# All cache pages fetched from the SP queue with the page number in a register

## The chip, the cores and the metric

The kernel runs on one core of a Trainium2 chip. The metric is the device time of one execution in microseconds (us); lower is better. Three runs of the kernel before gave 2349.99, 2351.92 and 2353.11 us, median 2351.92 us.

The engines are named as the profile names them: PE multiplies matrices (PEld is its weight load), DVE and ACT work element by element, POOL is the fourth compute engine, and SP computes nothing: its instruction queue (SPq) issues nearly all transfers between the chip's memory and the on-chip buffer. Every queue runs its instructions in order, so an instruction that waits holds up all that stands behind it on the same queue.

## What is computed

One step of a decoder layer for a prompt of 512 positions and 8 samples of 4 positions (544 columns together). The input is normalized and multiplied by one large projection; three branches (pooling, attention, state space) follow, each is projected back, and the results are gated, merged and projected out.

The change concerns the attention of the samples. Each sample has 2048 earlier positions in a paged cache: 16 pages of 128 positions, at places that a table of page numbers gives.

```python
past = cache_kv[l][page_table].reshape(bd, past_len, N_KV_ROWS, N_KV_HEADS, HEAD_DIM)
...
kc = jnp.einsum('bnlkd,lde->bnke', blk[:, :, :, 0] + pe_cmp[0][:, None, :], w_phi[0])
vc = jnp.einsum('bnlkd,lde->bnke', blk[:, :, :, 1] + pe_cmp[1][:, None, :], w_phi[1])
...
ss = jnp.einsum('bqkgd,bkqjcd->bkgqjc', qx, kg).astype(f32) * scale
...
o_sel = jnp.einsum('bkgqjc,bkqjcd->bqkgd', ps.astype(vg.dtype), vg)
```

A page has four tables: two for the compressed keys and values (`c0`, `c1`), and keys and values for the selected blocks (`ck`, `cv`). So 8 samples x 16 pages x 4 tables = 512 page fetches of 128 rows x 1 KB (128 KB) each.

## The kernel before

The dense work is a list of units, each one 128x1024 block of weights. `step` (L167) runs one unit: first it takes one turn of each background generator, then the evacuation of the previous unit, then `w_split` of the unit two ahead (ACT makes a rounded copy `whi` of the raw weights `wr`, DVE the rest `wlo`, L144 and L145), then `w_load` (L133: SP fetches the 512 KB of a unit three beyond that into one of 3 buffers `wr`), and then the unit's matmuls: 48 in a unit of the input projection, three for each product (L149 to L151). The kernel is scheduled by hand: every queue gets its instructions in the order in which the Python code issues them.

The attention work is one long background generator, taken in turns by the steps. Two of its parts read the cache, both through `gather(dst, table, col)`, where `col` numbers the 128 pages:

- `g_compress` (L604) goes through 16 jobs (8 samples, keys and values). A job's tile `ca` holds 16 pages; there are two such tiles. In three steps a job does 2 x 32 pairs of small matmuls (L632), and the pages of the next job (6, 5 and 5 of them in the three steps) are fetched into the other tile.
- `g_decode` (L1286) works through 20 chunks: for each of 4 pairs of samples four chunks of four cached pages per sample, and one chunk of the window, which is no paged fetch (L1307, L1318). For keys `gk` and values `gv` there are 4 buffers each, which is two chunks. `get_k` is called behind the score matmuls of a chunk (L1431) and fetches two chunks ahead; `get_v` is called behind the matmuls with the values (L1514) and does the same. A chunk with pages is 8 fetches. In the middle of the decode one step has both: 16 fetches.

`gather` splits the pages: an odd page goes over SP (L585 loads the page number from the on-chip row `PT` into a register, L586 issues a plain transfer whose address uses it), an even page goes over POOL as an indirect DMA (L589), which reads one row number for each partition from the table `IDX`. `make_idx` (L592) builds `IDX` at the start: POOL an iota, SP a transfer of the page table to all partitions, DVE four conversions.

In the SP queue a step's fetches stand ahead of the step's `w_load`, since the background turn comes first.

Of the kernel before, what the change touches and what calls it, by code (L numbers as in the profile page):

```python
# [10 lines left out]
F32 = mybir.dt.float32  # L11
F32R = mybir.dt.float32r
I32 = mybir.dt.int32
AF = mybir.ActivationFunctionType
OP = mybir.AluOpType
# [13 lines left out]
NPOOL = 160  # L29
# [37 lines left out]
def kernel(ctx, tc, a):  # L67
    nc = tc.nc
    pe, dve, act, pool, sp = nc.tensor, nc.vector, nc.scalar, nc.gpsimd, nc.sync
    ctx.enter_context(tc.manual_schedule())  # L70

    def P(name, bufs=1, **kw):
        return tc.tile_pool(name=name, bufs=bufs, **kw)
# [5 lines left out]
    consts = ctx.enter_context(P("consts"))  # L79
# [36 lines left out]
    ones = consts.tile([128, 128], F32, name="ones")  # L116
    epsb = consts.tile([128, 1], F32, name="epsb")

    # ---------------------------------------------------------------- dense stream
    raw, whi, wlo = {}, {}, {}  # L120
    lo_eng = [dve]
    early = [False]
# [36 lines left out]
    state = {"u": 0}  # L159
# [37 lines left out]
            fn()  # L197
            mid.pop(0)

    # ---------------------------------------------------------------- start: x, first weights  # L200
    xr_s = ExitStack()
    xr_p = xr_s.enter_context(P("xr"))
    XH, XL, XR = [], [], []
    first = wraw_p.tile([128, 8, 128], F32, name="wr")
# [98 lines left out]
            after.append(lambda hf=hf: rms_spread(hf))  # L303
        xr_s.close()

    # ---------------------------------------------------------------- pools of the first part
    att_s = ExitStack()
    kc_p = att_s.enter_context(P("kc", side="right"))
    KC = kc_p.tile([128, 2, 8, 64], F32, name="kc")
# [3 lines left out]
    KN = kc_p.tile([128, 2, 2, 32], F32, name="kn")  # L313
    GQ = kc_p.tile([128, 4, 48], F32, name="gq")

    # ---------------------------------------------------------------- evacuation of in-projection tiles
    done = set()
    sub = {}

# [256 lines left out]
                later(lambda t=t, i=2 * gi + md: sp.dma_start(ypool[i], t))  # L576
        step(u, mms, evac)

    # ---------------------------------------------------------------- compressed keys and values
    IDX = consts.tile([128, 128], I32, name="idx")  # L580
    PT = consts.tile([1, 128], I32, name="ptrow")

    def gather(dst, table, col):
        if col % 2:
            r = sp.value_load(PT[0:1, col:col + 1], min_val=0, max_val=NPOOL - 1)  # L585
            sp.dma_start(dst, a[table].rearrange("(g p) x -> g p x", p=128)[bass.ds(r, 1)]  # L586
                         .rearrange("g p x -> (g p) x"))
        else:
            pool.indirect_dma_start(out=dst, out_offset=None, in_=a[table],  # L589
                                    in_offset=bass.IndirectOffsetOnAxis(ap=IDX[:, col:col + 1], axis=0))  # L590

    def make_idx():  # L592
        pi = consts.tile([128, 1], I32, name="pidx")
        pool.iota(pi, pattern=[[0, 1]], base=0, channel_multiplier=1)
        pf = consts.tile([128, 1], F32, name="pidxf")
        dve.tensor_copy(pf, pi)
        sp.dma_start(PT, a["pt"])
        sp.dma_start(IDX, a["pt"].to_broadcast([128, 128]))
        f = consts.tile([128, 128], F32, name="idxf", bufs=1)
        dve.tensor_copy(f, IDX)  # L600
        dve.tensor_scalar(f, f, 128.0, pf, op0=OP.mult, op1=OP.add)
        dve.tensor_copy(IDX, f)

    def g_compress():  # L604
        with ExitStack() as s:
# [8 lines left out]
            def fetch(n, pages):  # L614
                if n >= len(jobs):
                    return
                b, k = jobs[n]
                if n not in tiles:
                    tiles[n] = cap.tile([128, 16, 256], F32, name="ca")
                for pg in pages:  # L620
                    gather(tiles[n][:, pg, :], f"c{k}", b * 16 + pg)
# [52 lines left out]
                dve.tensor_scalar(KCP[:, k, :16], KCP[:, k, :16], KCP[:, k, 16:17], None, op0=OP.add)  # L674
                dve.tensor_scalar(KC[:, k], KC[:, k], KCP[:, k, 16:17], None, op0=OP.add)

    # ---------------------------------------------------------------- state space
    SSM = {}
    par_s = ExitStack()

# [343 lines left out]
        par_s.close()  # L1024
        done.add("ssm")

    # ---------------------------------------------------------------- attention of the prompt
    def g_prompt():
        while not all(("q", i) in done for i in range(8)):
            yield  # L1030
# [251 lines left out]
        s.close()  # L1282
        done.add("prompt")

    # ---------------------------------------------------------------- attention of the samples
    def g_decode():  # L1286
        s = ExitStack()
        dp = s.enter_context(R("dec", 2))
# [10 lines left out]
        def get_k(r, c):  # L1299
            for b2 in range(2):  # L1300
                b_ = 2 * r + b2
                t = gp.tile([128, 4, 2, 128], F32, name="gk")
                if c < 4:
                    for pg in range(4):
                        gather(t[:, pg].rearrange("q p t -> q (p t)"), "ck", b_ * 16 + c * 4 + pg)
                else:
                    sp.dma_start(t.rearrange("q a b c -> q (a b c)"), a["wkT"][b_].rearrange("q p t -> q (p t)"))  # L1307
                kt[r, c, b2] = t

        def get_v(r, c):  # L1310
            for b2 in range(2):
                b_ = 2 * r + b2
                t = gp.tile([128, 4, 256], F32, name="gv")
                if c < 4:
                    for pg in range(4):
                        gather(t[:, pg], "cv", b_ * 16 + c * 4 + pg)
                else:
                    sp.dma_start(t, a["wv"][b_])  # L1318
                vt[r, c, b2] = t
# [222 lines left out]
        s.close()  # L1542
        done.add("decode")

    # ---------------------------------------------------------------- operands of the branches
    YH, YL = {}, {}
    yps = {}

# [59 lines left out]
                yz[k] = (y, z)  # L1608
            yield

    # ---------------------------------------------------------------- run the first part
    make_idx()

    def g_copy():
        while "ssm" not in done:
# [58 lines left out]
            fn()  # L1674
    xs.close()

    # ---------------------------------------------------------------- branches
    acc_p = ctx.enter_context(P("accp", 17))
    lg_p = ctx.enter_context(P("lgp", 3))
    xo_p = ctx.enter_context(P("xo", 24))  # L1680
# [157 lines left out]
    normalize(1, range(16))  # L1838


# ------------------------------------------------------------------------------ host side
def col_lists():
    off = np.cumsum([0, 1024, 1024, 1024, 1536, 48, 1024, 1024, 1024, 6144])
    pu, pz, q, kv, ag, az, su, sz, mg = off[:9]
    hd = []
    for p in range(2):
        for g in range(4):
            hd.append(np.concatenate([((2 * p + k) * 4 + g) * 64 + np.arange(64) for k in range(2)]))
    ssm = []
    for i in range(8):  # L1850
        c, g = np.meshgrid(np.arange(2 * i, 2 * i + 2), np.arange(64), indexing="ij")
        ssm.append((g * 16 + c).reshape(-1))
    agc = []
    for j in range(3):
        for p in range(2):
            for g in range(4):
                for k in range(2):
                    agc.append(((2 * p + k) * 4 + g) * 3 + j)
    r = np.arange(128)
    return dict(hd=hd, ssm=ssm, cols={  # L1860
        "pu": [pu + 128 * i + r for i in range(8)], "pz": [pz + 128 * i + r for i in range(8)],
        "q": [q + h for h in hd], "az": [az + h for h in hd],
        "kv": [kv + 128 * i + r for i in range(12)],
        "ag": [ag + np.array(agc + [agc[0]] * 80)],
        "su": [su + s for s in ssm], "sz": [sz + s for s in ssm],
        "mg": [mg + 128 * i + r for i in range(48)]})
# [138 lines left out]
```

## Time and profile before

| | |
|---|---|
| median of the timed runs | 2351.92 us (2349.99 to 2353.11) |
| span of the profiled execution | 2475.4 us |
| PE busy | 2345.3 us, 95% of the span |
| DVE, ACT, POOL busy | 1111.0, 652.3, 419.9 us |
| mean granted clock of PE | 0.965 |
| POOL's indirect DMAs | 256 |
| SP's page fetches | 256 |

No other time than the span is recorded for the profiled execution. The span is 123.5 us longer than the median of the timed runs. A row of a timeline gives the start, how long, the queue or engine, the line, the operation, what was written from what, how many were merged (x4), and in brackets the idle time before it and what ended it. "issue" is idle time for which the profile shows nothing that was waited for. In a row of the windows view each engine's busy time is followed by the number of its instructions, then come the granted clock (PEclk), the DMA share and GB/s.

### The profile page before, as it was taken

Reading aid. Unit: us, or ns where it says so; the run is one execution under the profiler, and the core shown is the slowest. Engines: PE = TensorE matmul, PEld = TensorE weight load, DVE = VectorE, ACT = ScalarE, POOL = GpSimd, SP = SyncE. Lnnn points to the kernel's source line nnn. Section 1 sums busy time; section 2 is a strip of 40 time slices with the busy share of each in tenths; the row PEclk is TensorE's granted clock in tenths of the full one; section 3 lists DMA queues with packets and bytes.
Section 4 is the critical chain, followed back from the end, with each engine's and each line's share of the span. In section 5 each row is a group of like instructions: output and inputs, shape, how many; then the busy total and the mean of one; then the engine's idle time right before and its main releaser. Section 6 shows DMA issues by size and latency. Waiting matters only on the chain.

```text
span 2475.4 us, 49565 instructions
## 1 busy us (share of the span) xinstructions
PE 2345.3 (95%) x20454; PEld 2236.5 (90%) x20454; DVE 1111.0 (45%) x2157; ACT 652.3 (26%) x1117; POOL 419.9 (17%) x387
## 2 busy tenths in 40 slices
PE   8888888999978999999999999889999999999995
PEld 7888888899978999999999898779999999999995
DVE  6223334114498324676666333322452545554225
ACT  5101111112311111444544222222342222222331
POOL 3122222213235200000000214551000001200003
PEclk9898989999999999999999999999999999999998
DMA  7554564546323666533333357775553555443332
GB/s 241 153 128 125 136 165 124 149 120 137 106 80 108 143 195 195 168 91 96 100 92 87 121 156 246 239 220 170 189 136 118 170 194 191 145 131 111 113 110 91
DMA packets 271650, 358.32 MB, mean 145 GB/s; under 512 B 136129, under 2 KB 186050, under 8 KB 271042
## 3 DMA queue, kind: packets, MB, share of 16 engines
q1 hardware_dynamic: 259138, 321.60, 44.0%
q0 software_dynamic: 12288, 33.57, 4.9%
q8 instruction: 161, 2.64, 0.4%
q14 instruction: 63, 0.52, 0.1%
HBM read 309.26 MB, written 54.13 MB: 147 GB/s over the span
## 4 chain that ended last, share of the span: by engine, by line
PE 89%; DVE 5%; issue 4%; DMA 1%; SPq 0%; ACT 0%; POOL 0%; DVEq 0%; POOLq 0%; ACTq 0%
PE d L149 25%; PE d L151 23%; PE d L150 23%; PE s L632 5%; PE o L1244 2%; PE s L1180 2%; PE t L1220 2%; PE o L1514 1%; DVE t L902 1%; DVE sh L905 1%; PE s L1431 1%; DVE t L904 1%; PE s L963 1%; DVE t L903 1%; PE s L974 1%
## 5 line engine op out<-in xcount | busy, mean ns | idle before, releaser
L149 PE MATMUL d<-xh,whi 128*128 128x272 f32 x3424 | 1022.2, 299 | 24.4 <-DVE e L324 13.4
L151 PE MATMUL d<-xl,whi 128*128 128x272 f32 x3424 | 998.3, 292 | 9.0 <-issue 8.7
L150 PE MATMUL d<-xh,wlo 128*128 128x272 f32 x3424 | 998.1, 291 | 4.5 <-issue 4.0
L149 PEld LDWEIGHTS d<-xh,whi 128*128 128x128 f32 x3424 | 659.7, 193 | 55.7 <-issue 33.2
L151 PEld LDWEIGHTS d<-xl,whi 128*128 128x128 f32 x3424 | 658.9, 192 | 9.1 <-issue 8.0
L150 PEld LDWEIGHTS d<-xh,wlo 128*128 128x128 f32 x3424 | 659.9, 193 | 5.7 <-issue 5.0
L145 DVE TENSOR_TENSOR wlo<-wr,whi 128x1024 fp32r<-128x1024 f32 x298 | 376.8, 1265 | 302.6 <-ACT whi L144 292.9
L144 ACT ACTIVATE whi<-wr 128x1024 fp32r<-128x1024 f32 x309 | 323.0, 1051 | 534.2 <-PE d L151 425.5
L324 DVE TENSOR_TENSOR e<-d,rstd 128x272 f32<-128x272 f32 x186 | 81.6, 439 | 502.5 <-PE d L151 369.6
L589 POOL DMA_INDIRECT ca<-c,idx x128 | 126.8, 990 | 362.3 <-PE s L632 277.9
L632 PE MATMUL s<-ca,wphi 128*64 128x64 f32 x2048 | 141.5, 290 | 46.3 <-issue 39.3
L632 PEld LDWEIGHTS s<-ca,wphi 128*64 128x64 f32 x2048 | 118.6, 158 | 65.6 <-issue 61.1
L589 POOL DMA_INDIRECT gk<-ck,idx x64 | 65.6, 1024 | 622.0 <-ACT e L426 557.0
L151 PE MATMUL d<-ml,whi 128*128 128x272 f32 x512 | 148.1, 289 | 0.0
L149 PE MATMUL d<-yhA,whi 128*128 128x272 f32 x512 | 147.9, 289 | 0.0
L150 PE MATMUL d<-mh,wlo 128*128 128x272 f32 x512 | 147.7, 288 | 0.0
L149 PE MATMUL d<-mh,whi 128*128 128x272 f32 x512 | 147.7, 288 | 0.0
L151 PE MATMUL d<-ylA,whi 128*128 128x272 f32 x512 | 147.6, 288 | 0.0
L150 PE MATMUL d<-yhA,wlo 128*128 128x272 f32 x512 | 147.3, 288 | 0.0
L151 PE MATMUL d<-ylB,whi 128*128 128x272 f32 (+2 forms) x384 | 110.8, 288 | 0.0
L149 PE MATMUL d<-yhB,whi 128*128 128x272 f32 (+2 forms) x384 | 110.7, 288 | 0.0
L150 PE MATMUL d<-yhB,wlo 128*128 128x272 f32 (+2 forms) x384 | 110.5, 288 | 0.0
(391 smaller groups left out, 2861.7 us busy)
## 6 DMA issues: line engine op xcount, KB each, us to landing
wr<-wd SPq DMA_DIRECT2D x309, 512.0 KB
ca<-c SPq DMA_DIRECT2D x128, 128.0 KB
gates<-e SPq DMA_DIRECT2D x48, 272.0 KB
lg<-gates SPq DMA_DIRECT2D x48, 272.0 KB
gk<-ck SPq DMA_DIRECT2D x64, 128.0 KB
gv<-cv SPq DMA_DIRECT2D x64, 128.0 KB
xo<-xT SPq DMA_DIRECT2D x32, 136.0 KB
yT<-yo SPq DMA_DIRECT2D x32, 136.0 KB
```

What stands on the lines that cost most here:

```text
L144: act.activation(hi, r, AF.Copy)
L145: lo_eng[0].tensor_tensor(lo, r, hi.bitcast(F32), op=OP.subtract)
L149: pe.matmul(ps, lhsT=h, rhs=xh, start=start, stop=False)
L150: pe.matmul(ps, lhsT=l, rhs=xh, start=False, stop=False)
L151: pe.matmul(ps, lhsT=h, rhs=xl, start=False, stop=stop)
L324: dve.tensor_tensor(out[:, cols(hf)], ps[:, :HALF], rstd[:, cols(hf)], op=OP.mult)
L589: pool.indirect_dma_start(out=dst, out_offset=None, in_=a[table], in_offset=bass.IndirectOffsetOnAxis(ap=IDX[:, col:col + 1], axis=0))
L632: pe.matmul(acc_b[kv2 * 64:(kv2 + 1) * 64, :64], lhsT=wphi[:, k, d, :], rhs=t[:, :, kv2, d], start=(d == 0), stop=(d == 31))
L902: m(t1_, A8[:, 0], prev, op=OP.mult)
L1180: pe.matmul(st[n][k][:, off:off + nk], lhsT=QS[pg][k][:, qt * 128:(qt + 1) * 128], rhs=KS[br, k][j][:, :nk], start=(j == 0), stop=(j == 1))
L1220: pe.transpose(b[:, c:c + 128], st[n][k][:, c:c + 128], ident)
L1244: pe.matmul(o[hs[k], qt * 128:(qt + 1) * 128], lhsT=VN[:, kb, br, pg // 4, hs[k]], rhs=st[n][k][:, off + kb * 128:off + (kb + 1) * 128], s ...
```

## The change

`gather` loses the distinction: all 512 page fetches go over SP, each with a register load and a plain transfer. `make_idx` is gone, with `IDX`, the iota, four DVE instructions and one SP transfer; the load of `PT` stands where it was. Comment lines are gone too, so that lines behind them have lower numbers (L586 becomes L584, L133 stays).

```diff
-    IDX = consts.tile([128, 128], I32, name="idx")
     PT = consts.tile([1, 128], I32, name="ptrow")
 
     def gather(dst, table, col):
-        if col % 2:
-            r = sp.value_load(PT[0:1, col:col + 1], min_val=0, max_val=NPOOL - 1)
-            sp.dma_start(dst, a[table].rearrange("(g p) x -> g p x", p=128)[bass.ds(r, 1)]
-                         .rearrange("g p x -> (g p) x"))
-        else:
-            pool.indirect_dma_start(out=dst, out_offset=None, in_=a[table],
-                                    in_offset=bass.IndirectOffsetOnAxis(ap=IDX[:, col:col + 1], axis=0))
...
+        r = sp.value_load(PT[0:1, col:col + 1], min_val=0, max_val=NPOOL - 1)
+        sp.dma_start(dst, a[table].rearrange("(g p) x -> g p x", p=128)[bass.ds(r, 1)]
+                     .rearrange("g p x -> (g p) x"))
...
-    make_idx()
+    sp.dma_start(PT, a["pt"])
```

In the two places below the order of instructions is shown as it stands in the built programs. The first is the SP queue at the start of `g_compress`, behind the load of its weights `wphi`. Before, two page fetches (a register load, three register instructions, a transfer) stand ahead of the first write of `u_p`:

```order
L608 DMA wphi<-wphi 128x4096
L585 TENSOR_LOAD ptrow
L585 ISA x2
L586 ISA
L586 DMA ca<-c 128x256
L585 TENSOR_LOAD ptrow
L585 ISA x2
L586 ISA
L586 DMA ca<-c 128x256
L447 DMA u_p<-e_689 128x8x64
```

With the change the same place begins as follows, and `u_p` comes behind the fourth fetch:

```order
L591 DMA wphi<-wphi 128x4096
L583 TENSOR_LOAD ptrow
L583 ISA x2
L584 ISA
L584 DMA ca<-c 128x256
L583 TENSOR_LOAD ptrow
L583 ISA x2
L584 ISA
L584 DMA ca<-c 128x256
L583 TENSOR_LOAD ptrow
L583 ISA x2
L584 ISA
```

What moved: each group of fetches on SP has twice as many, and nothing else on that queue changed its place; in the whole program SP has 1874 rows of this kind before and 2897 with the change. The second place is the POOL queue in the decode, ahead of the branches (`eq` is a product in the block selection, `acc` the merging of the branches). Before:

```order
L951 COPY bd_8744<-bb 64x8x16 x2
L589 DMA gk<-ck,idx 128x256 x8
L589 DMA gv<-cv,idx 128x256 x8
L1386 TENSOR_TENSOR eq<-eq,tie 128x900
L589 DMA gk<-ck,idx 128x256 x20
L589 DMA gv<-cv,idx 128x256 x4
L589 DMA gk<-ck,idx 128x256 x4
```

With the change:

```order
L934 COPY bd_9886<-bb 64x8x16 x2
L1369 TENSOR_TENSOR eq<-eq,tie 128x900
L1699 TENSOR_TENSOR acc<-acc,lg 128x544 x16
L1790 TENSOR_TENSOR yo<-yo,rstd 128x272 x2
L1792 TENSOR_TENSOR yo<-yo,xo 128x272 x2
```

What moved: POOL's 128 fetches of the decode are gone from here, as its 128 fetches of `g_compress` are further ahead. On PE and ACT the order of instructions is the same as before; DVE lacks the four conversions.

## Rows read from the trace of the kernel before

**Rows 1.** The page, part 1: span, then busy time, share and instructions of each engine.

```profile
span 2475.4 us, 49565 instructions
...
PE 2345.3 (95%) x20454; PEld 2236.5 (90%) x20454; DVE 1111.0 (45%) x2157; ACT 652.3 (26%) x1117; POOL 419.9 (17%) x387
```

**Rows 2.** Windows (PE, PEld, DVE, ACT, POOL): the compression, and the decode's fetches.

```profile
48.00:541.00 493.00, 438.66 (x4095) 411.45 (x4095) 140.40 (x334) 62.28 (x87) 123.31 (x126) 0.90 0.55 146
...
1470.00:1693.00 223.00, 204.96 (x1998) 173.15 (x1991) 70.13 (x106) 52.63 (x78) 117.23 (x112) 0.94 0.75 230
```

**Rows 3.** SP's timeline in the decode: page fetches, a weight load, a window load.

```profile
1429.00 4.10 SPq L586 DMA_DIRECT2D gk<-ck  x4
1433.20 0.37 SPq L133 DMA_DIRECT2D wr<-wd  x1
1434.35 3.70 SPq L586 DMA_DIRECT2D gk<-ck  x4
...
1470.62 3.90 SPq L586 DMA_DIRECT2D gk<-ck  x4
...
1538.69 0.82 SPq L1318 DMA_DIRECT2D gv<-wv  x2
```

**Rows 4.** Lines 585 and 586: SP's instructions, duration in ns (least/median/most).

```profile
L585 SPq TENSOR_LOAD <-ptrow x256: 3/268/1281, 47.3 to 1691.0; - x128
L585 SPq FUSED_REGOPS  x256: 2/152/711, 47.8 to 1691.3; - x128
...
L586 SPq FUSED_REGOPS  x256: 3/42/700, 48.2 to 1691.5; - x128
...
L586 SPq MOVE gk<-ck x64: 3/29/727, 1428.9 to 1644.2; - x64
L586 SPq DMA_DIRECT2D gk<-ck x64: 3/333/700, 1429.0 to 1644.2; - x64
```

**Rows 5.** PE's timeline in the decode: score matmuls, and the transposes of the last step.

```profile
1515.09 1.06 PE L1431 MATMUL s<-gk,qbd 128*32 128x512 f32 x8
...
1538.48 1.04 PE L1431 MATMUL s<-gk,qbd 128*32 128x512 f32 x8
...
1547.09 1.04 PE L1431 MATMUL s<-gk,qbd 128*32 128x512 f32 x8
...
1701.81 0.60 PE L1482 MATMUL t<-ident,S 128*128 128x128 f32 x4
```

**Rows 6.** Line 1431: score matmuls, duration in ns, first and last start in us.

```profile
L1431 PE MATMUL s<-gk,qbd x160: 592/593/1062, 1469.5 to 1663.8; 128*32 128x512 f32 x160
```

**Rows 7.** ACT's timeline: first use of the first 128 KB of weights, issued at 0.76.

```profile
2.91 0.42 ACT L249 ACTIVATE whi<-wr 128x256 fp32r<-128x256 f32 x1 [0.87 <-DMA wr<-wd]
```

**Rows 8.** PE's waits (total us, times, longest), 84 to 545 us; then 545 to 1400 us.

```profile
PE s L632 <- issue: 39.3, 67, 1.1
...
PE d L149 <- DVE e L324: 13.4, 5, 4.8
```

**Rows 9.** POOL's timeline, then PE's, in the decode's first burst of indirect DMAs.

```profile
1400.35 1.02 POOL L589 DMA_INDIRECT gk<-ck,idx  x1 [556.99 <-ACT e L426]
...
1420.21 0.95 POOL L589 DMA_INDIRECT gv<-cv,idx  x1 [0.31 <-issue]
...
1418.42 0.39 PE L151 MATMUL d<-xl,whi 128*128 128x272 f32 x1 [1.12 <-issue]
```

**Rows 10.** PE's timeline: the small matmuls of two neighbouring compression steps.

```profile
310.98 2.66 PE L632 MATMUL s<-ca,wphi 128*64 128x64 f32 x44
...
319.75 2.43 PE L632 MATMUL s<-ca,wphi 128*64 128x64 f32 x40
```

**Rows 11.** SP's waits (total us, times, longest), 48 to 541 us.

```profile
SPq L133 <- DVE wlo L145: 118.2, 26, 12.8
SPq L133 <- DVE pe_p L463: 52.0, 5, 13.4
```

**Rows 12.** PE's longest wait at the start, 10 to 50 us.

```profile
PE t L150 <- DVE wlo L145: 1.2, 1, 1.2
```

More of the change, by code (lines that the diff above doesn't have):

```diff
@@ L577, in pool_unit @@
         step(u, mms, evac)
-    IDX = consts.tile([128, 128], I32, name="idx")
     PT = consts.tile([1, 128], I32, name="ptrow")
     def gather(dst, table, col):
-        if col % 2:
-            r = sp.value_load(PT[0:1, col:col + 1], min_val=0, max_val=NPOOL - 1)
-            sp.dma_start(dst, a[table].rearrange("(g p) x -> g p x", p=128)[bass.ds(r, 1)]
-                         .rearrange("g p x -> (g p) x"))
-        else:
-            pool.indirect_dma_start(out=dst, out_offset=None, in_=a[table],
-                                    in_offset=bass.IndirectOffsetOnAxis(ap=IDX[:, col:col + 1], axis=0))
[L592 to L602, printed above, removed]
+        r = sp.value_load(PT[0:1, col:col + 1], min_val=0, max_val=NPOOL - 1)
+        sp.dma_start(dst, a[table].rearrange("(g p) x -> g p x", p=128)[bass.ds(r, 1)]
+                     .rearrange("g p x -> (g p) x"))
     def g_compress():
```

## The prediction

> **What bounds the kernel now.** I read the page's busy times first: PE is busy for 95% of 2475.4 us and POOL for 17% [rows 1], so a change to POOL's queue can only matter through what PE waits for. Next come the windows [rows 2]. POOL's page fetches lie in two stretches, the compression (48 to 541 us) and the decode (1470 to 1693 us). [...]
>
> [...] PE's list of waits between 84 and 545 us is nearly all "issue", 39.3 us in 67 gaps, at the small matmuls of the compression; between 545 and 1400 us, where POOL fetches nothing, its first entry is an ordinary wait for DVE and no "issue" stands in the list [rows 8]. The timeline shows the same: PE gaps of about 1 us come late in a burst of POOL's indirect DMAs, here 18 us into the one that runs from 1400.35 to 1421.2 us [rows 9]. So the gaps go with POOL's bursts. But SP is held up in the same way: its register instructions, 29 to 152 ns in the median, take up to 700 to 727 ns, and others of 268 and 333 ns are recorded with 3 ns [rows 4]. A transfer that is issued in 3 ns is no real issue time. It looks like records that come out in clumps, and that points to the recording as what holds the engines. The sizes fit too: the span is 123.5 us above the median of the timed runs. The 54.3 us of idle time in the compression and the 37 us that I find below for the decode are 91 us, and the low clock can add up to 49 us (0.10 of 493 us; less, as gap and low clock overlap). 91 to 140 us brackets 123.5 us. I take it that timed runs have hardly any of these gaps, and do my sums without them.
>
> [...]
>
> **The price of a fetch on SP.** Four fetches in a row take 3.70 us from the first issue to the end of the fourth [rows 3]; with 0.34 us for the last transfer that leaves 3.36 us for three spacings, 1.12 us each. The lower end is the sum of the medians of a fetch's five larger instructions, 268 + 152 + 42 + 29 + 333 ns = 0.82 us [rows 4], nothing between them. The upper end is the other group of four, 4.10 us, which gives 1.25 us. I take 1.12 us, since fetches in a row are what the change makes more of.
>
> [...]
>
> **The decode: the term that decides.** Count the SP queue from the seventh step of the decode's fetches, issued from 1470.62 us [rows 3], to its last paged fetch. In the code's order there are 14 key and 14 value chunks of 8 fetches: 224, of which POOL had 112. Beside them stand 22 weight loads at 0.37 us, 11 writes of gates at about the same, and 7 window loads at 0.82 us [rows 3]; that is 18 us, with some 0.1 us between them 22 us.
> - Before, SP needs 112 x 1.12 + 22 = 147 us.
> - After, it needs 224 x 1.12 + 22 = 273 us.
>
> What PE needs over the same steps: the score matmuls begin at 1469.5 us [rows 6] and the sixth following step's at 1515.09 us [rows 5], 45.6 us without a gap. Thirteen more steps lead to the last score matmuls at 1663.8 us. A step free of gaps takes 8.61 us there (1538.48 to 1547.09 us [rows 5]), so 111.9 us, where the trace has 148.7: that is the 37 us of holding. The last five steps, to the transposes at 1701.81 us that the last paged values follow, take 38.0 us. Sum 195.5 us. So before, SP's 147 us fit beside PE's 195.5 us. After, 273 us do not: SP becomes the bound. The buffers can't hide it. They hold two chunks, so a fetch must have landed two steps after it was allowed, and in a step with both chunks SP needs 2 x 8 x 1.12 + 0.4 = 18.3 us against PE's 8.61 us. Weight loads stand behind the fetches in each step, but a unit's weights are fetched five units ahead, so their delay of some two steps costs nothing of its own; nor do the writes of gates.
>
> SP begins the first register load at about 1469.8 us, ends at 1469.8 + 273 = 1742.8, and the last page lands within 1.8 us (the first 128 KB of weights, issued from 0.76 to 1.15 us, were used at 2.91 us [rows 7]): 1744.6 us, or 275 us after 1469.5. Against 195.5 us this is **+80 us**. With 0.82 us a fetch it is 184 + 22 + 2 - 195.5 = +13 us, with 1.25 us it is 280 + 22 + 2 - 195.5 = +109 us.
>
> **The compression: covered.** Here 128 fetches x 1.12 = 143 us move to SP. A job's three steps take 3 x 8.77 = 26.3 us free of gaps (310.98 to 319.75 us [rows 10]); SP then needs 16 x 1.12 = 17.9 us, 1.1 us of weight loads and some 3 us for the pooling's transfers, 22 us. Its cover is time it now spends waiting for the weight split, 118.2 and 52.0 us [rows 11]. The next job's pages may start as soon as the other tile is read, some 6 us before the job begins (a step of 8.77 less its 2.66 us of small matmuls [rows 10]), so none is late: 0. Jobs with a short pooling unit have only 23 us, and the very first job gets its second half from SP instead of from a POOL that started early; each may be late by a few us, 0 to 20 us together.
>
> **The rest.** The four DVE conversions stand ahead of two weight splits at the start; PE's longest wait there is 1.2 us for such a split [rows 12], so -1.2 to 0 us. POOL's queue ahead of the block selection empties, which can only let its product there start earlier: 0.
>
> **Sum.** Without the gaps the profiled execution would be 2475.4 - (91 to 140) = 2335 to 2384 us, about the timed median, so I add the terms to that median: 2351.92 + 80 + 0 = **2432 us**. The profile of the changed kernel should have neither the gaps nor the low clock: 2335 to 2384 + 80 = 2415 to 2464 us, a span slightly shorter than 2475.4 although the timed runs are slower.
>
> **Rivals.**
> - **The gaps are real** (faster). If POOL's bursts hold PE in the timed runs as in the profile, the change frees 54 to 103 us in the compression (idle time alone, or with the low clock), while the decode goes from the recorded 232.3 us (1469.5 to 1701.81) to 275 us, +43 us. Net -11 to -60 us: 2292 to 2341 us, about 2320. For it: the low clock shows that PE really stood still. Against it: the 123.5 us, and the 3 ns records. It decides the sign as soon as more than 80 of the 91 to 140 us are in the timed runs.
> - **Hidden** (same). If a fetch costs SP 0.77 us or less, 224 x 0.77 + 22 + 2 fits in 195.5 us, and the time stays at 2352. Against it: five of its instructions alone sum to 0.82 us.
> - **Cheap fetches** (slower, less). Back-to-back issue without recording at 0.82 to 1.0 us: +13 to +53 us, 2365 to 2405.
> - **Both stretches** (slower, more). If the compression also falls behind by 10 to 20 us on top of the 80: 2442 to 2452, and up to 2461 with 1.25 us a fetch.
>
> **How the numbers follow.** SP-bound decode at about 1.12 us: 0.57, with 2405 to 2461 as its own range. Cheap fetches 0.15; both stretches 0.08; hidden 0.05; gaps real 0.15. The range of 8 in 10 takes in all the slower cases and half of "hidden": 2350 to 2461; outside are the faster case and a small rest. A measurement of this kernel tells about 0.2% (4.7 us) from no change. Slower 0.80, same 0.05, faster 0.15.
>
> **What would show it.** Right: SP's fetches in the decode in unbroken rows of 8 and 16 at 1.12 us with hardly a wait between 1470 and the end; PE waiting in each full step for `gk` or `gv`, and a step of some 18 us; about 275 us from the first score matmuls to the last paged values; no "issue" gaps at L632's successor; POOL silent there. Wrong: SP still waiting in the decode (the fetch is cheaper), or the timed median falling together with the span (the gaps were real), or new waits of PE for `ca` in the compression.

## The result, and the profile after

| | kernel before | changed kernel |
|---|---|---|
| median of the timed runs | 2351.09 us (2349.99 to 2353.11) | 2451.22 us (2447.76 to 2453.8) |
| ratio | | 1.0424, 95% interval 1.0409 to 1.0438 |
| span of the profiled execution | 2475.4 us | 2452.0 us |
| busy POOL | 419.9 us | 161.0 us |

The changed kernel is 100 us slower, where 80 were forecast. The span fell by 23 us all the same, as forecast. The forecast had taken the gaps of the first profile for a thing of the recording that times don't show; that turned out wrong, and much of what follows is about it.

The page of the changed kernel (span, then busy time, share and instructions of each engine; the last two rows are the chain that ended last, by engine and by line):

```profile
span 2452.0 us, 50447 instructions
...
PE 2325.2 (95%) x20454; PEld 2214.9 (90%) x20454; DVE 1108.6 (45%) x2153; ACT 653.7 (27%) x1117; POOL 161.0 (7%) x130
...
PE 82%; SPq 7%; DVE 5%; issue 3%; DMA 2%; ACT 0%; POOL 0%; DVEq 0%; ACTq 0%; POOLq 0%
PE d L149 23%; PE d L151 22%; PE d L150 22%; PE s L615 4%; SPq L583 3%; SPq L584 3%; PE s L1163 2%; PE o L1227 2%; PE t L1203 2%; DVE t L885 1%; DVE sh L888 1%; DVE t L886 1%; PE s L946 1%; DVE t L887 1%; PE s L1414 1%
```

SP's two lines of a fetch, L583 and L584, now stand on the chain with about 6% of the span. They are instructions of a queue that computes nothing. The same queue in the decode, as a timeline:

```profile
1442.55 8.58 SPq L584 DMA_DIRECT2D gv<-cv  x8
1451.96 8.48 SPq L584 DMA_DIRECT2D gk<-ck  x8
1460.55 0.37 SPq L133 DMA_DIRECT2D wr<-wd  x1
1461.75 8.14 SPq L584 DMA_DIRECT2D gv<-cv  x8
```

Sixteen fetches stand behind one another with nothing between them, then one weight load and the next eight, all at 1.12 to 1.18 us each. PE's waits of the same stretch (1388 to 1688 us; total us, times, longest) and two of them in the timeline:

```profile
PE s L1414 <- DMA gk<-ck: 46.3, 14, 4.2
PE s L1414 <- DMA gk<-wkT: 4.8, 4, 1.6
PE o L1497 <- DMA gv<-cv: 3.8, 7, 0.7
```

```profile
1457.39 1.92 PE L1414 MATMUL s<-gk,qbd 128*32 128x512 f32 x4 [3.99 <-DMA gk<-ck]
1462.22 1.92 PE L1414 MATMUL s<-gk,qbd 128*32 128x512 f32 x4 [2.91 <-DMA gk<-ck]
```

PE waits for the key tile of a chunk's first sample (3.99 us), does four matmuls, and waits again for that of the second (2.91 us). No "issue" gap is left in PE's waits.

### The profile page after: what moved, and what is told of

Same layout as the page of the kernel before. It is cut to its first block, busy times and chain, and to the rows that moved or that the text cites. A ratio compares the mean times of both kernels' runs of the same rounds, so it can differ in the third digit from the quotient of the medians.

```text
span 2452.0 us, 50447 instructions
## 1 busy us (share of the span) xinstructions
PE 2325.2 (95%) x20454; PEld 2214.9 (90%) x20454; DVE 1108.6 (45%) x2153; ACT 653.7 (27%) x1117; POOL 161.0 (7%) x130
## 4 chain that ended last, share of the span: by engine, by line
PE 82%; SPq 7%; DVE 5%; issue 3%; DMA 2%; ACT 0%; POOL 0%; DVEq 0%; ACTq 0%; POOLq 0%
PE d L149 23%; PE d L151 22%; PE d L150 22%; PE s L615 4%; SPq L583 3%; SPq L584 3%; PE s L1163 2%; PE o L1227 2%; PE t L1203 2%; DVE t L885 1%; DVE sh L888 1%; DVE t L886 1%; PE s L946 1%; DVE t L887 1%; PE s L1414 1%
## 5 line engine op out<-in xcount | busy, mean ns | idle before, releaser
L615 PE MATMUL s<-ca,wphi 128*64 128x64 f32 x2048 | 123.9, 289 | 19.7 <-DMA ca<-c 17.7
L615 PEld LDWEIGHTS s<-ca,wphi 128*64 128x64 f32 x2048 | 112.5, 154 | 27.4 <-issue 21.7
L149 PEld LDWEIGHTS d<-mh,whi 128*128 128x128 f32 x512 | 96.4, 188 | 0.0
L151 PEld LDWEIGHTS d<-ylA,whi 128*128 128x128 f32 x512 | 96.4, 188 | 0.0
```

Of the source, the lines that this page charges most:

```text
L149: pe.matmul(ps, lhsT=h, rhs=xh, start=start, stop=False)
L151: pe.matmul(ps, lhsT=h, rhs=xl, start=False, stop=stop)
L615: pe.matmul(acc_b[kv2 * 64:(kv2 + 1) * 64, :64], lhsT=wphi[:, k, d, :], rhs=t[:, :, kv2, d], start=(d == 0), stop=(d == 31))
```

## The kernel before again: where its gaps were

The kernel before, unchanged, was profiled once more (diff: none), since its first span did not fit its times.

> The kernel before once more, unchanged, to see what its own executions give as span and as time. Theory (the 'issue' gaps belong to the recording of POOL's bursts): executions timed at about 2351 us have spans of about 2349 us and a granted clock above 0.97, while the profiled one is again some 120 us longer at about 0.965. Rival (the gaps are real): every execution that has a span shows about 2475 us, or the timed ones vary up to it.

Its median was 2352.82 us, and the profiled execution took 2352.59 us with a span of 2350.8 us, so the span is 1.8 us short of the time. Every other execution with both has a span 1.7 to 3.4 us below its time. Of the theory the spans of about 2349 us came, but not a profiled execution some 120 us longer; nor did the rival's 2475 us. Page, windows (the columns of [rows 2]) and waits of this profile:

```profile
span 2350.8 us, 49565 instructions
...
PE 2286.4 (97%) x20454; PEld 2199.1 (94%) x20454; DVE 1110.3 (47%) x2157; ACT 652.8 (28%) x1117; POOL 419.5 (18%) x387
```

```profile
48.00:541.00 493.00, 480.56 (x4916) 463.34 (x4915) 173.37 (x371) 82.41 (x126) 150.77 (x147) 0.99 0.62 166
1377.00:1586.00 209.00, 208.39 (x2212) 183.28 (x2210) 74.24 (x111) 56.89 (x85) 116.12 (x112) 1.00 0.82 262
```

```profile
PE d L149 <- DVE e L324: 15.1, 6, 4.8
PE s L632 <- DMA wr<-wd: 8.0, 1, 8.0
PE t L1016 <- POOL bd L951: 4.8, 1, 4.8
...
PE s L1431 <- issue: 0.6, 1, 0.6
```

Between 48 and 1700 us there is one "issue" gap of 0.6 us, where [rows 8] has 39.3 us in the compression alone. POOL's burst is the same as in [rows 9]; here its first and last DMA, and behind them what PE did in those 20.36 us (window):

```profile
1318.98 1.03 POOL L589 DMA_INDIRECT gk<-ck,idx  x1 [556.96 <-ACT e L426]
...
1338.38 0.96 POOL L589 DMA_INDIRECT gv<-cv,idx  x1 [0.30 <-issue]
```

```profile
1318.98:1339.34 20.36, 20.36 (x195) 20.10 (x194) 4.91 (x6) 5.98 (x10) 15.78 (x16) 1.00 0.82 250
```

PE worked through the whole burst. SP's records are whole too; compare with [rows 4], where the least is 3 ns and the most 700 ns and above:

```profile
L586 SPq FUSED_REGOPS  x256: 37/42/48, 48.8 to 1566.9; - x128
L586 SPq MOVE gk<-ck x64: 29/29/42, 1336.3 to 1525.3; - x64
L586 SPq DMA_DIRECT2D gk<-ck x64: 332/333/482, 1336.4 to 1525.3; - x64
```

So the same program, recorded by the same profiler, with the same bursts, runs with the gaps and without. Neither the bursts nor the recording make them by themselves. PE has its 20454 matmuls in the same order in every kernel here, so the start of the n-th can be set beside the start of the n-th of another profile. The table gives the start in this profile, and how much later it is in others:

| n-th matmul, where it stands | before, no gaps | before, first profile | changed kernel | four numbers a load (below) |
|---|---|---|---|---|
| 400, ahead of the small matmuls | 60.3 us | +8.9 | -0.4 | -0.6 |
| 800, the first of the 16 jobs done | 105.4 | +5.6 | +4.4 | -2.4 |
| 4400, compression nearly over | 457.8 | +82.5 | +10.9 | -0.9 |
| 11600, ahead of the decode's fetches | 1294.7 | +81.4 | +10.8 | -1.5 |
| 12400, first score matmuls done | 1383.8 | +92.2 | +10.8 | -1.5 |
| 14400, about the last transposes | 1573.1 | +124.6 | +101.4 | +8.6 |
| 20400, end | 2319.0 | +124.6 | +101.2 | +8.5 |

The first profile lost 124.6 us, all of them in the stretches in which POOL issues indirect DMAs, and none in between. The changed kernel loses 10.9 us in the compression and 90.6 us in the decode. So the profile without gaps is the one to set the changed kernel's beside.

## The two halves of the change

Decode alone: `gather` gives SP every page of `ck` and `cv`, and splits the others as before.

```diff
-        if col % 2:
+        if col % 2 or table in ("ck", "cv"):
```

> Half of the change: all pages of the decode (ck, cv) over SP, the compression split as before. Theory (the decode is bound by SP's 1.12 us per fetch and carries nearly all of the loss): +80 us as forecast, up to +90, so 2431 to 2441 us; in the profile the compression keeps its 'issue' gaps and its low clock, so that the span stays above the time by 50 to 90 us. Rival (both stretches lose): +40 to +60, the rest being the compression's. If the gaps are real: +43, about 2395.

Measured: 2439.77 us beside 2353.25 us, ratio 1.037 (1.0352 to 1.0387), +86.5 us. Compression alone, with `("c0", "c1")` in the same place:

> The other half: all pages of the compression (c0, c1) over SP, the decode split as before. Theory: the gaps in the compression go from the profile, PE waits some 18 us for ca instead as in the profile of the changed kernel, and the timed run is 10 to 20 us slower, 2362 to 2372 us, while the span falls by some 40 us. Rival (the gaps are real): 40 to 100 us faster, 2250 to 2311. If the compression is covered as the prediction had it: 2352.

Measured: 2363.66 us, ratio 1.0058 (1.0037 to 1.0079), +10.4 us. The halves sum to 96.9 us, the whole change to 99 to 100. What the decode alone did to PE, in its score matmuls (least/median/most ns, first and last start) and its waits; then the score matmuls of the kernel before without gaps; then PE's waits in the compression alone:

```profile
L1431 PE MATMUL s<-gk,qbd x160: 589/617/1062, 1374.8 to 1622.2; 128*32 128x512 f32 x160
```

```profile
PE s L1431 <- DMA gk<-ck: 44.5, 13, 4.2
```

```profile
L1431 PE MATMUL s<-gk,qbd x160: 589/592/617, 1377.4 to 1539.3; 128*32 128x512 f32 x160
```

```profile
PE s L632 <- DMA ca<-c: 20.2, 5, 6.7
```

Without gaps the score matmuls take 161.9 us from the first to the last, with the decode's fetches on SP 247.4. The expectation for the decode alone that the compression would keep its gaps and the span stay above the time fell: this group of runs had none to keep (span 2436.1 us for 2437.84 us).

## Is it SP's issue time?

The changed kernel with the decode's fetches at fixed addresses, on the same queue. It leaves out the page table there, so it reads other pages and its result isn't the layer's; number, sizes and order of the transfers stay.

```diff
     def gather(dst, table, col):
+        if table in ("ck", "cv"):
+            sp.dma_start(dst, a[table].rearrange("(g p) x -> g p x", p=128)[col])
+            return
```

> The changed kernel, but in the decode each fetch reads the page at a fixed number (col), a plain transfer without a register load: it leaves out the page table there, so other pages are read; transfers, queue, order and sizes stay. Theory (SP's issue time is the bound): a fetch costs about 0.4 us as a weight load does, SP needs 224 x 0.4 + 22 = 112 us against PE's 195, and the decode's loss goes: 2352 plus the 10 to 20 us of the compression, 2362 to 2372. Rival (one queue instead of two, or the transfers themselves, bound the decode): 2430 to 2450 as the changed kernel.

Measured: 2364.96 us beside 2353.25 us, ratio 1.005 (1.0033 to 1.0067). Of the changed kernel's 98 us beside this 2353.25, 86 are gone with the register instructions, although all 512 transfers still go over SP. PE's waits for keys shrink from 46.3 us to 1.6 us, and those for `ca` stay, as the compression is left alone:

```profile
PE s L1417 <- DMA gk<-ck: 1.6, 2, 1.3
...
PE s L618 <- DMA ca<-c: 14.8, 5, 7.8
```

One queue instead of two costs nothing measurable in the decode, then (11.7 us are left in all, and the compression alone cost 10.4); the register instructions ahead of each transfer do, 86 us. That other pages are read could still have a part in it. The next kernel settles that: it reads the right pages, keeps the register-held addresses and makes them cheaper: one load brings four page numbers, and the assertion on their bounds is left out.

```diff
-        r = sp.value_load(PT[0:1, col:col + 1], min_val=0, max_val=NPOOL - 1)
+    def numbers(col, n):
+        return nc.values_load_multi_w_load_instructions(
+            PT[0:1, col:col + n], [mybir.EngineType.SP], min_val=0, max_val=NPOOL - 1,
...
-                    for pg in range(4):
-                        gather(t[:, pg], "cv", b_ * 16 + c * 4 + pg)
+                    for pg, rg in enumerate(numbers(b_ * 16 + c * 4, 4)):
+                        gather(t[:, pg], "cv", rg)
```

> The changed kernel, but one register load brings four page numbers, and the assertion on their bounds is left out: per fetch there stay two register instructions and the transfer, 0.09 + 0.07 + 0.39 us, and a quarter of a load, 0.08, with the semaphore 0.04 more: 0.63 to 0.67 us. Theory (SP's time per fetch decides): SP needs 224 x 0.67 + 26 = 176 us in the decode, under PE's 200, and half of the time in the compression: 2355 to 2365 us on either kind of chip, so within 0.5% of the kernel before on one, 4.5% faster on the other. Rival (register-held addresses cost beyond SP's instructions): above 2400.

Measured: 2362.74 us beside 2354.28 us, ratio 1.0044 (1.0027 to 1.0061), as expected. Its rows: SP's instructions, two groups of eight fetches, and PE's wait in the decode:

```profile
L583 SPq TENSOR_LOAD <-ptrow x158: 271/301/2427, 47.4 to 1574.2; - x158
```

```profile
L587 SPq FUSED_REGOPS  x512: 37/37/51, 47.9 to 1576.5; - x171
```

```profile
1449.64 4.37 SPq L587 DMA_DIRECT2D gv<-cv  x8
1454.61 5.11 SPq L587 DMA_DIRECT2D gk<-ck  x8
```

```profile
PE s L1420 <- DMA gk<-ck: 4.2, 4, 1.8
```

158 loads instead of 512, and eight fetches mostly in 4.4 to 5.1 us instead of 8.1 to 8.8. The compression's loss is gone (the table above has -0.9 us at the 4400th matmul); some 10 us are left in the decode, against the expectation that SP's time would hide there. PE's waits make up 5.6 of them (4.2, with 1.0 and 0.4 for other tiles); the rest stays open. A repeat:

> The variant with four page numbers to a register load once more, beside the kernel before. Theory (it issues no indirect DMA, so nothing holds it on any chip, and SP's 0.65 us per fetch hide): 2360 to 2368 us wherever it runs; beside a kernel before at 2470 to 2477 that is a ratio of 0.955 to 0.957, beside one at 2353 again 1.003 to 1.006. Rival (such a chip holds SP's fetches too): 2450 and more there.

Measured: 2363.12 us beside 2350.09 us, ratio 1.0056 (1.004 to 1.0073). A kernel before with gaps was not met in this group.

## The gaps, in groups of runs that have them

The runs come in groups, each with the kernel before among them. In four groups the kernel before had medians of 2350 to 2354 us; in two it had 2470 and 2477 us, and there every run of it lay between 2465.96 and 2482.35 us. No profile of the kernel before is kept from these two. That it has the gaps there is read from its spans (2464 to 2481 us) and its granted clock (0.964 to 0.969), which are the first profile's (2475.4 us, 0.965), and from the kernels that ran in one of the two: POOL fetches for the compression in three of the four, and these have the first profile's gaps there (PE's "issue" time at the small matmuls is 38.5, 37.9 and, with twice the fetches on POOL, 114.5 us). The first kernel moves the opposite way: all of the compression's pages on POOL.

```diff
-        if col % 2:
+        if col % 2 and table in ("ck", "cv"):
```

> The opposite edit: the compression's 256 fetches all on POOL as indirect DMAs, the decode split as before. Theory (POOL's bursts cost the timed run nothing): POOL needs 16 x 1.26 = 20 us of a job's 26 us, so 2353, at most 10 us off either way. Rival (POOL's bursts hold PE): twice the bursts, 40 us and more slower.

Measured: 2631.17 us beside 2476.7 us, ratio 1.0615 (1.0574 to 1.0655), +154.5 us. The theory on record, that the bursts cost timed runs nothing, falls for this group. Its page, and PE's waits from 48 to 760 us:

```profile
PE 2391.9 (91%) x20454; PEld 2266.2 (86%) x20454; DVE 1110.5 (42%) x2157; ACT 652.8 (25%) x1117; POOL 550.2 (21%) x515
```

```profile
PE s L632 <- issue: 114.5, 142, 2.4
PE d L151 <- issue: 16.5, 13, 3.8
PE d L149 <- issue: 15.8, 20, 1.7
```

128 indirect DMAs more tripled the "issue" time at the small matmuls from [rows 8]'s 39.3 us. In this group, where POOL fetches more, PE stands still more.

The second kernel takes POOL out and gives ACT the decode's even pages:

```diff
-        r = sp.value_load(PT[0:1, col:col + 1], min_val=0, max_val=NPOOL - 1)
-        sp.dma_start(dst, ...
+        q = act if table in ("ck", "cv") and col % 2 == 0 else sp
+        r = q.value_load(PT[0:1, col:col + 1], min_val=0, max_val=NPOOL - 1)
+        q.dma_start(dst, ...
```

> The changed kernel, but in the decode the even pages are fetched from ACT's queue (same register load and plain transfer), the odd ones from SP: POOL issues nothing, and every fetch is register-held. Theory: SP fits again (112 x 1.175 + 26 = 158 of 200 us). ACT has 132 us of fetches beside some 66 us of work in 200 us, which is just full, and its fetches wait for PE ahead of its own splits: the decode loses 10 to 40 us, with the compression's 10 that is 2373 to 2403, clearly below the changed kernel's 2451. Rival (register-held fetches as such are slow, from whatever queue): 2440 and more.

Measured: 2416.08 us beside 2476.7 us, ratio 0.9753 (0.9732 to 0.9774), 13 us above the expected range and 35 us below the changed kernel. There is no "issue" gap in it, in a group whose kernel before is full of them. What is late instead are ACT's own products, behind its fetches, and what DVE makes of them (PE's waits, 1386 to 1645 us):

```profile
PE t L1466 <- DVE S L1446: 15.2, 3, 6.3
PE o L1498 <- ACT dpt L1480: 9.0, 4, 3.2
PE s L1415 <- ACT S L1432: 7.9, 2, 3.9
```

Two more were meant as doses of SP time in the decode: a second, unused load ahead of each SP fetch of the kernel before, and three pages of four on SP (`if col % 2 or (col % 4 and table in ("ck", "cv"))`).

> The kernel before, but in the decode SP loads a second page number (unused) ahead of each of its 112 fetches; no transfer is added, moved or changed, and POOL keeps its 112. Theory (SP's instruction time alone is the bound): a load with its register operation and assertion adds about 0.59 us, so SP needs 112 x (1.175 + 0.59) + 26 = 224 us in the decode against the 200 us that PE took there in the clean profile of the kernel before: +24 us, 2377 (2368 to 2384). Rival (what binds is that all transfers go through one kind of queue): 2353.

> The kernel before, but in the decode SP has three pages of four and POOL one. Theory: SP needs 168 x 1.175 + 26 = 223 us against 200: +23 us, 2376 (2368 to 2384), a quarter of the whole move's loss for half of the moved fetches, since the first part fits in SP's spare time. Rival (a loss for each fetch moved): half of the 86 us, 2396.

Measured: 2503.42 us, ratio 1.0105 (1.0084 to 1.0126), +26.7 us; and 2467.81 us, ratio 0.9962 (0.995 to 0.9975), -8.9 us. The first lies at the expected +24 us, the second missed its +23 us. Both expectations took PE's 200 us without gaps. In the first kernel's decode PE has 16.6 us of "issue" gaps (1464 to 1735 us), and SP's fetches of keys are recorded with 3 to 719 ns; in the second, with 64 fewer of POOL's DMAs, the gaps are 1.8 us (1300 to 1760 us), and PE waits 18.2 us for keys. By the matched matmuls (11600 to 14400) the two lost 70.7 and 37.8 us in the decode, the first profile 43.2 us. So they prove nothing about SP's time by themselves.

The last question was the change itself beside a kernel before with gaps. It was run twice more:

> The changed kernel once more, beside the kernel before on the same chip. On the last chip the kernel before took 2476.7 us in the timed runs, with the same gaps as in the first profile; on the one ahead of it 2353. Theory now (POOL's bursts of indirect DMAs hold the engines on some chips and not on others; the changed kernel has none): 2451 on either, so a ratio of 0.99 where the kernel before takes 2477, and 1.042 where it takes 2352. Rival (that chip is slower in general): 1.04 on both, so 2575 there.

> The changed kernel and the kernel before on one chip again, for the question that is still open: whether the sign of the change goes with the chip. Theory: the changed kernel takes 2451 to 2456 us whatever the kernel before takes, so a ratio of 1.042 beside 2352, and of 0.99 beside 2477. Rival (the chip on which the kernel before took 2477 is slower in general): 1.04 on both, 2575 there.

The first met a group without gaps: 2453.4 us beside 2354.28 us, ratio 1.043 (1.0412 to 1.0447). The second met one with them: 2451.71 us beside 2469.98 us, ratio 0.9925 (0.9908 to 0.9941). Span and PE's wait in that profile:

```profile
span 2451.5 us, 50447 instructions
```

```profile
PE s L1414 <- DMA gk<-ck: 47.6, 15, 4.3
```

The changed kernel takes the same time in both, and shows the same waits. The rival on record, a chip that is slower in general, would have given 2575 us beside 2470 to 2477. It is the kernel before that moves by 118 us. So **the sign of this change depends on the group**: 4.2% slower beside a kernel before without gaps, as in the runs of the result, and 0.75% faster beside one with them.

What makes a group one or the other is open. It isn't the number of the chip that the runs carry: the group of the second repeat and that of the repeat with four numbers a load carry the same one, with 2469.98 and 2350.09 us for the kernel before. All executions here have spans and so are recorded, so the runs can't tell whether the recording has a part in the gaps.

## Why the prediction came out as it did

**The gaps: right for the sum, wrong in the reason.** "I take it that timed runs have hardly any of these gaps" held for the timed runs shown, so the median was the right number to add the terms to. The step that failed is the one before it, from the 3 ns records and the 123.5 us to "the recording is what holds the engines", something that belongs to one profiled execution. The runs showed a recorded execution without gaps (2350.8 us) and timed runs at 2466 to 2482 us. So the first profile most likely comes from a situation like that of these two groups, and the 123.5 us are the difference of two situations; this is inferred, since its own time isn't recorded. The median on record told the prediction which situation to reckon with; beside the other one +80 us would have had the direction wrong (-18.3 us measured). The bracket of 91 to 140 us was good (54.3 us of it are 493.00 less 438.66 us in [rows 2], and its 49 us are the 0.10 that the clock of 0.90 there lacks): the matched matmuls give 124.6 us, and put them into the two stretches that the prediction named (82.5 and some 43 us).

**The rival "gaps are real"** fits the two groups of six that have them. It gave -11 to -60 us where all of the gaps are in the timed runs; measured in the one of the two in which the change ran: -18.3 us. Its times, 2292 to 2341 us, took off from a median without gaps and didn't come: 2451.71 us. The low clock that spoke for it follows a pause in the first profile: PE is busy for 27 to 32% of each microsecond from 301 to 305 us, and the granted clock is 0.50 from 306 to 309 us.

**The price of a fetch: right in size.** 1.12 us was forecast. It was read from the shortest of SP's groups of four, so it is a price without mishaps. In the decode of the changed kernel the median from one register load to the next instruction behind the transfer is 1.11 us, and the mean 1.175 us (224 fetches in 263.3 us), since some 25 fetches took 0.2 to 0.6 us longer (a load or a transfer of 0.5 to 0.9 us instead of 0.27 and 0.33, or a pause between two instructions), and one waited 3.0 us.

**The decode: right mechanism, term too small.** Forecast +80 us, measured +90.6 us in the profile and +86.5 us alone. From the first score matmuls to the last transposes the changed kernel takes 290.7 us (forecast 275), the kernel before without gaps 200.2 us (forecast 195.5), by these rows of the two:

```profile
L1414 PE MATMUL s<-gk,qbd x160: 589/617/1063, 1388.2 to 1638.4; 128*32 128x512 f32 x160
```

```profile
L1465 PE MATMUL t<-ident,S x80: 271/272/273, 1424.5 to 1678.9; 128*128 128x128 f32 x80
```

```profile
L1482 PE MATMUL t<-ident,S x80: 270/272/276, 1413.3 to 1577.6; 128*128 128x128 f32 x80
```

Of the 15.7 us that the changed kernel's stretch was longer, about 12 us are the mean of 1.175 instead of 1.12 us, and about 4 us the other transfers (26 instead of 22 us). The 195.5 us were put together from gap-free steps out of a profile with gaps and came out 4.7 us short.

**The low clock was said to go, and came back elsewhere.** The compression's did rise (0.90 in [rows 2], 0.99 in the profile without gaps, 0.98 now), but in the decode it is lower than in either profile of the kernel before (0.94 and 1.00):

```profile
48.00:541.00 493.00, 473.29 (x4801) 456.37 (x4801) 168.59 (x367) 79.56 (x118) 19.86 (x17) 0.98 0.62 164
...
1388.00:1688.00 300.00, 243.28 (x2220) 194.70 (x2219) 74.51 (x111) 59.28 (x87) 0.00 (x0) 0.87 0.60 189
...
1456.00:1465.00 9.00, 4.70 (x12) 1.37 (x13) 0.79 (x2) 0.00 (x0) 0.00 (x0) 0.50 0.50 162
```

The last row of these windows of the changed kernel lies about the waits of 3.99 and 2.91 us shown above: the granted clock is 0.50 there, where it is 1.00 from 1440 to 1442 us. In the whole decode PE is busy for 243.3 us with what took it 208.4 us at a clock of 1.00. These 34.9 us and the waits shown above (54.9 us) together make up the stretch's loss of some 90 us. I take the slower matmuls for no loss of their own: SP's queue sets the end of the stretch, and PE only waits less for being slower. SP waits for PE for only some 7 us there, most of it in the row below (SP's waits, 1386 to 1680 us), which supports this; no run tests it alone.

```profile
SPq L584 <- PE o L1497: 4.0, 4, 3.0
```

**The compression: 0 with up to 20 allowed, measured 10.9 us.** One of the terms named there was right: the first job, whose second half comes from SP instead of a POOL that started early, costs 4.4 us, and the other jobs 6.5 us together. PE's waits at the small matmuls rose from 11.3 us (8.0, 1.9 and 1.4 us in the profile without gaps) to 19.5 us, which is 8.2 of the 10.9 us; the rest I can't place. New waits for `ca`, 17.7 us where the profile without gaps has 1.4, were on the prediction's own list of signs of being wrong. With them it is the rival "both stretches" (2442 to 2452 us, chance 0.08) that describes the outcome best, though the decode gave more than its 80 us as well; the main case's own range, 2405 to 2461 us, holds it too.

```profile
PE s L632 <- DMA ca<-c: 1.4, 1, 1.4
```

```profile
PE s L615 <- DMA ca<-c: 17.7, 4, 7.8
PE s L615 <- DMA pe_s<-poolT: 1.8, 1, 1.8
```

```profile
SPq L133 <- DVE wlo L145: 47.3, 15, 8.2
```

The first row is of the profile without gaps. The last is SP's wait for the weight split, 118.2 us before [rows 11] and 115.8 us in the profile without gaps: most of the cover is used up, not all.

**The rival "hidden"** needed 0.77 us or less for a fetch, and the mean is 1.175 us. With fixed addresses, where a fetch is one transfer of 0.43 us in the median, all of them on one queue cost nothing measurable in the decode, where PE waits 1.6 us for keys. SP's time for register-held addresses doesn't stay hidden: it is worth 86 us.

## What to carry to other kernels

Add up what a queue issues, per instruction and not per transfer, and set it beside what the engine behind it needs in the same stretch: a queue that computes nothing was the bound here at 1.175 us per 128 KB, and cost the decode some 10 us instead of 90 at about 0.6 us, with four page numbers to a load. Before a change is judged by a profile, see that the profile belongs to the times: a span that was 5% off the timed median was here another situation of the same program, not a detail of one profiled execution. The kernel before ran in two situations, at 2350 to 2354 and at 2470 to 2477 us, between which the change alters its sign; in such a case the variant that is safe in both is worth more than the best of one. Here that may be four numbers a load, which gives up 0.4 to 0.6% beside the kernel before without gaps; that it keeps its time beside one with gaps is not shown, only that the changed kernel, which has no indirect DMAs either, did.

## What the runs showed of the hardware that was not expected

- In bursts of POOL's indirect DMAs PE and SP stood still, PE for up to 1.1 us at a time at the small matmuls of the first profile (39.3 us in 67 gaps) and up to 3.8 us with all of the compression's pages on POOL, SP for some 0.7 us (700 to 727 ns for instructions of 29 to 152 ns in the median [rows 4]). The profile without gaps has 0.6 us of it between 48 and 1700 us; the same program takes 2477 or 2351 us. Not every burst in such a group does it: with three of the decode's pages in four on SP, PE's gaps were 37.9 us in the compression and 1.8 us in the decode. What brings this about is open. The step from 128 to 256 such DMAs in the compression cost 154.5 us there, more than the first 128, which cost 82.5 us in the first profile (by the matched matmuls, at the 4400th; 74.0 and 76.7 us in the two kernels of that group that left the compression as before).
- One register load of four numbers took SP 301 ns in the median, one of a single number 268 ns.
- The same register and transfer instructions on ACT's queue, half of the decode's fetches beside ACT's own work, cost the decode some 50 us (58.5 us by the matched matmuls, less 8.9 us from the compression), although ACT's own work is only 58.55 of 259 us there: ACT's idle share was no room for the fetches, behind which its own products came late (PE waited 9.0 and 7.9 us for them).
